# A table of expert gates built two tokens at a time instead of four, in a transformer block on one Trainium2 core

## The chip, the core and the metric

The kernel runs on one core of a Trainium2 chip. The core has a matrix engine (PE, with its weight loads shown as PEld), a vector engine (DVE), a scalar engine (ACT), GpSimd (POOL, here used only to issue DMAs) and a sync engine (SP, which issues the weight loads). Every engine works through its own instructions in order; they wait for each other on semaphores. The metric is the device time of one execution in microseconds, as the median of several runs. Before the change it is 2024.65 us (three runs, 2024.57 to 2025.96).

## What is computed

One transformer block for 256 tokens of width 2048, in float32: a modulated norm, a mixer (attention and a gated recurrence), then a feed-forward layer of 16384 experts of which each token uses 8 x 16 = 128. Only the last part matters here:

```python
q = (hf @ wq).reshape(T, PEER_HEADS, 2, PEER_DQ // 2)
s = jnp.einsum('thpd,hpkd->thpk', q, keys)        # two scores of 128 keys for each head
v1, i1 = lax.top_k(s[:, :, 0], 16); v2, i2 = lax.top_k(s[:, :, 1], 16)
vals, pick = lax.top_k(v1[..., :, None] + v2[..., None, :], 16)   # expert = 128 * i1 + i2
g = jax.nn.softmax(vals, axis=-1)
act = gelu(x_c @ down[e_c]) * g_c                 # for the 128 picked experts of a token
out = act @ up[e_c]
```

## The kernel before

The kernel doesn't gather experts. It multiplies all tokens with all 16384 rows of `down` (32 blocks `d` of 512 experts), takes the gelu, multiplies with a dense gate table that is zero where an expert was not picked, and multiplies the result with all of `up` (16 groups `u`). For this each float32 weight is split into a high and a low part in a shorter format: ACT casts `raw` to `wh` (L209), DVE subtracts to get `wl` (L210), and PE multiplies three times (L375 to L377 for `d`, L358 to L360 for `u`). One such split (128 x 1024 values) and the 24 matmuls of 256 columns (`d`), or 12 of 512 (`u`), that use it are called a round here. There are three buffers each for `wh` and `wl`. So the split for round n can only start when PE has finished round n-3, and runs while PE is in round n-2. Rounds 0 to 31 make the queries `wq`, rounds 32 to 191 are the first 20 `d` blocks (eight rounds each), round 192 is the first of `u`.

The gate table `wd` in DRAM is built by `w_build` while PE works on the first 20 `d` blocks. For each token DVE makes two one-hot rows of 128 (`oh`, L1198), one for each half of the expert number; the first is scaled by the high and low part of the gate (`ga`, by ACT in L1228 and by DVE in L1225); PE multiplies the second with them (`w`, L1218), which gives 128 x 256 sums for a token. These are taken out of PSUM by ACT (L1209, high part) and DVE (L1210, adds the low part) into `stg`, of which there is one buffer. Every 32 tokens `stg` is stored to `wd` by a DMA of 2 MB (L1212, issued by POOL). Each step makes four tokens. A token's sums take half a PSUM bank; there are four banks for them (three with the tag `t`, one with the tag `p`), thus for two steps of four tokens.

The order of work is written by generators. After every round `tick` advances them: a job of priority 0 (the gelu of a `d` block, `ev_d`, two steps, once in eight rounds) comes first; the table has priority 3 and gets the rate in the last place of `RATES` for each round, but in the round in which `ev_d` is at the head, two steps are run, and the second of them runs on into the table. A scheduler then sets each engine's order from priorities and its own durations. Before block 19 (round 184) all steps that are left are emitted, the memory of the table's tiles is given back, and the first two blocks of gates are asked for: `act_load` issues `wt` (gates, read from `wd`, L1250) and `xS` (gelu values stored earlier in `xd`, L1247) on POOL; `act` multiplies them on DVE (L1260, four parts of 128 x 256) and splits the product into `ah` (ACT) and `al` (DVE), which the rounds of `u` need. `xT` and `xS` share three buffers, `wt` has two.

Of the kernel before, what the change touches and what calls it, by code (L numbers as in the profile page):

```python
# [8 lines left out]
F32R = mybir.dt.float32r  # L9
# [3 lines left out]
OP = mybir.AluOpType  # L13
AX = mybir.AxisListType

P = 128
D = 2048
S = 256
# [10 lines left out]
NEB = NE // 512  # L29
NUG = NE // 1024  # L30
LAG = 20
RATES = (2, 1.8, 0.7, 0.51)
WK = 0
ADG = 9
RG = 2
# [15 lines left out]
GPLACE = 48  # L51
# [19 lines left out]
def kernel(  # L71
# [24 lines left out]
    V, A, T, G = nc.vector, nc.scalar, nc.tensor, nc.gpsimd  # L96
# [12 lines left out]
    def ps_t(name):  # L109
        return ps[0].tile([P, 512], F32, tag="t", bufs=ps[2], name=name)  # L110
# [20 lines left out]
    iota = con[:, C_IOTA:C_IOTA + P]  # L131
# [21 lines left out]
    for ch in STREAM.replace(" ", ""):  # L153
# [6 lines left out]
        else:  # L160
            src, o = wid[ch].pop(0)
# [184 lines left out]
    def tick(n=1):  # L346
        tk[0] += min(n, RATES[jobs[0][0]]) if jobs and (jobs[0][0] < 3 or wn[0] > WK) else n
        while tk[0] >= 1:
            tk[0] -= 1
            step()  # L350
# [156 lines left out]
    for which, i0, i1 in SEGS:  # L507
# [11 lines left out]
        if not sums[which]:  # L519
            if which == "f":  # L520
                t = [vp.tile([P, 2, NT, 512], F32, tag="av", bufs=ADAB, name=f"part{i}") for i in range(2)]
                sums["f"] = [[t[b // 2][:, b % 2, tb] for tb in range(NT)] for b in range(4)]
            else:
                t = sqp.tile([P, 4, NT, 512], F32, name="sums")
# [534 lines left out]
    for i in range(8):  # L1059
        t = x1T[:, 2 * i:2 * i + 2]  # L1060
# [19 lines left out]
    kq = e4.enter_context(tc.tile_pool(name="kq", bufs=1))  # L1080
    idT = kq.tile([P, S, 2], F32, name="idT")
# [97 lines left out]
        A.copy(idT[:, tbs[tb]].rearrange("p t i -> p i t"), tp[:, 0:2 * P].rearrange("p (i t) -> p i t", i=2))  # L1179
        A.copy(gT[:, tbs[tb]], tp[:, 2 * P:3 * P])  # L1180

    def turn_tile(tag, place, dt, name):

        t = kq.tile([P, 4 * 2 * P + (64 if place else 0)], dt, tag=tag, bufs=3, name=name)
        return t[:, place:place + 4 * 2 * P].rearrange("p (k o i) -> p k o i", k=4, o=2)

    def w_build():

        stg, ohs, gas, wps = {}, {}, {}, {}
        gl = kq.tile([P, S], F32, name="gl")  # L1190
        gh = kq.tile([P, S], F32R, name="gh")
        A.copy(gh, gT)
        V.tensor_tensor(gl, gT, gh.bitcast(F32), OP.subtract)
        for q in range(64 + 4):
            wn[0] = q
            if q < 64:
                oh = turn_tile("oh", 0, F32R, f"oh{q}")
                V.tensor_tensor(oh, iota.unsqueeze(1).unsqueeze(1).to_broadcast([P, 4, 2, P]),  # L1198
                                idT[:, 4 * q:4 * q + 4].unsqueeze(3).to_broadcast([P, 4, 2, P]), OP.is_equal)
                ohs[q] = oh  # L1200
            if 0 <= q - 4:
                p_, tg = q - 4, (q - 4) // 8
                if p_ % 8 == 0:
                    stg[tg] = kq.tile([P, P, 32], F32, tag="stg", bufs=1, name=f"stg{tg}")
                o = (p_ % 8) * 4
                for k, w in enumerate(wps.pop(p_)):
                    w4 = w.rearrange("p (k o i) -> p i o k", k=2, o=2)
                    d = stg[tg][:, :, o + 2 * k:o + 2 * k + 2]
                    A.copy(d, w4[:, :, 0])  # L1209
                    V.tensor_tensor(d, d, w4[:, :, 1], OP.add)  # L1210
                if p_ % 8 == 7:
                    G.dma_start(wd[tg], stg.pop(tg))  # L1212
            if 0 <= q - 3 < 64:
                p_ = q - 3
                oh, ga = ohs.pop(p_), gas.pop(p_)
                wps[p_] = [ps_t(f"w{p_}0"), (ps_p if p_ % 2 else ps_t)(f"w{p_}1")]
                for k in range(4):
                    T.matmul(wps[p_][k // 2][:, k % 2 * S:k % 2 * S + S], oh[:, k, 1], ga[:, k].rearrange("p o i -> p (o i)"),  # L1218
                             start=True, stop=True)
            if 0 <= q - 1 < 64:  # L1220
                p_ = q - 1
                ga = turn_tile("ga", GPLACE, F32R, f"ga{p_}")
                gas[p_] = ga
                hot = ohs[p_][:, :, 0].bitcast(F32)
                V.tensor_tensor(ga[:, :, 1], hot, gl[:, 4 * p_:4 * p_ + 4].unsqueeze(2).to_broadcast([P, 4, P]), OP.mult)  # L1225
                for k in range(4):
                    t = 4 * p_ + k
                    A.activation(ga[:, k, 0], hot[:, k], AF.Copy, scale=gh[:, t:t + 1].bitcast(F32))  # L1228
            yield

# [69 lines left out]
    for s in range(LAG):  # L1300
        if s == 0:
            finish(0)
            add(picks(0), 2)
            add(picks(1), 2)
            add(w_build(), 3)
        if s == LAG - 1:
            while jobs:
                step()
            e4.close()
            upp = ctx.enter_context(tc.tile_pool(name="upp", bufs=1))  # L1310
            acc = upp.tile([P, NT, D], F32, name="acc")
            for eb in range(2):
                act_load(eb, upp)
                add(act(eb, upp))
        add(ev_d(s, turned(f"d{s}", ticks=2)), 0)
# [124 lines left out]
```

## Time and profile before

| what | value |
|---|---|
| median of three runs | 2024.65 us |
| profiled execution, own time | 2027.09 us |
| its span | 2025.3 us |
| PE busy | 1953.6 us (96%) |
| DVE busy | 1529.3 us (76%) |
| ACT busy | 1024.1 us (51%) |
| POOL busy | 67.6 us (3%) |
| granted PE clock, mean | 0.983 |
| the table's products (L1218), first and last start | 664.4 to 1002.5 us |
| first matmul of `u` | 1057.12 us |

A busy PE is not PE at its peak, since matmuls are pipelined and their ends are modelled. So for PE the starts of the matmuls are read beside the busy share. Idle time of an engine that is not the bottleneck costs nothing; a wait counts when PE waits behind it.

### The profile page before, as it was taken

How to read it: one execution, taken by the hardware profiler on the slowest of the kernel's cores; microseconds unless marked ns; L12 is line 12 of the kernel's file. 1: busy time of each engine (PE TensorE's matmuls, PEld its weight loads, DVE VectorE, ACT ScalarE, POOL GpSimd, SP SyncE). 2: the span in 40 equal slices, each digit the busy share in tenths (PEclk: the TensorE clock that was granted, in tenths of full speed). 3: DMA queues.
4: the chain of work that ended last, by engine and by line, in shares of the span. 5: the costliest groups of instructions: out<-in, count | busy, mean ns of one | idle time of the engine just before them, and what ended most of it. 6: DMA issues, size and time to landing. Idle time of an engine off the chain costs nothing.

```text
span 2025.3 us, 30935 instructions
## 1 busy us (share of the span) xinstructions
PE 1953.6 (96%) x12346; PEld 1728.4 (85%) x12346; DVE 1529.3 (76%) x2342; ACT 1024.1 (51%) x1519; POOL 67.6 (3%) x107
## 2 busy tenths in 40 slices
PE   5999898898999999999999999999999999999998
PEld 4777565787999999999998888888899999999997
DVE  7888999887999888788757666666566666665566
ACT  3544676455445767677654444444344444444442
POOL 0000000000000000000011000000000000000000
PEclk7999998898999999999999999999999999999999
DMA  9898778895546676666798776775577777676563
GB/s 374 325 372 330 277 307 315 345 347 219 175 169 208 215 260 234 229 230 232 270 331 300 246 242 229 234 251 201 190 267 253 262 250 253 240 243 212 190 223 131
DMA packets 77600, 515.39 MB, mean 254 GB/s; under 512 B 8720, under 2 KB 9232, under 8 KB 21904
## 3 DMA queue, kind: packets, MB, share of 16 engines
q1 hardware_dynamic: 63792, 450.50, 62.0%
q0 software_dynamic: 13664, 62.92, 9.0%
q8 instruction: 96, 1.57, 0.3%
q14 instruction: 48, 0.39, 0.1%
HBM read 481.93 MB, written 31.46 MB: 253 GB/s over the span
## 4 chain that ended last, share of the span: by engine, by line
PE 75%; DVE 10%; issue 10%; DMA 3%; ACT 2%; POOL 1%; SPq 0%; DVEq 0%; POOLq 0%
PE u L359 11%; PE u L358 11%; PE u L360 11%; PE d L377 8%; PE d L376 8%; PE d L375 8%; DVE av L231 3%; DVE wl L210 3%; PE wq L375 2%; PE wq L376 2%; PE wq L377 2%; PE y L360 1%; PE y L358 1%; PE y L359 1%; DMA wd<-stg 1%
## 5 line engine op out<-in xcount | busy, mean ns | idle before, releaser
L210 DVE TENSOR_TENSOR wl<-raw,wh 128x1024 fp32r<-128x1024 f32 x649 | 789.3, 1220 | 374.7 <-ACT wh L209 372.0
L209 ACT CAST wh<-raw 128x1024 fp32r<-128x1024 f32 x649 | 680.2, 1051 | 768.5 <-PE u L360 364.2
L377 PE MATMUL d<-xH,wl 128*128 128x256 f32 x2048 | 568.4, 278 | 0.8 <-DVE wl L210 0.7
L375 PE MATMUL d<-xH,wh 128*128 128x256 f32 x2048 | 568.4, 278 | 0.0
L376 PE MATMUL d<-xL,wh 128*128 128x256 f32 x2048 | 567.9, 277 | 0.0
L359 PE MATMUL u<-wl,ah 128*128 128x512 f32 x1024 | 398.9, 390 | 1.3 <-DVE wl L210 1.3
L358 PE MATMUL u<-wh,ah 128*128 128x512 f32 x1024 | 398.7, 389 | 0.0
L360 PE MATMUL u<-wh,al 128*128 128x512 f32 x1024 | 398.4, 389 | 0.0
L377 PEld LDWEIGHTS d<-xH,wl 128*128 128x128 f32 x2048 | 385.3, 188 | 1.3 <-DVE wl L210 1.2
L376 PEld LDWEIGHTS d<-xL,wh 128*128 128x128 f32 x2048 | 385.2, 188 | 0.4
L375 PEld LDWEIGHTS d<-xH,wh 128*128 128x128 f32 x2048 | 385.2, 188 | 0.4
L359 PEld LDWEIGHTS u<-wl,ah 128*128 128x128 f32 x1024 | 192.2, 188 | 41.2 <-DVE wl L210 1.7
L360 PEld LDWEIGHTS u<-wh,al 128*128 128x128 f32 x1024 | 192.3, 188 | 40.2
L358 PEld LDWEIGHTS u<-wh,ah 128*128 128x128 f32 x1024 | 192.2, 188 | 39.7
L231 DVE SCALAR_TENSOR_TENSOR av<-av,cb 128x2048 f32<-128x2048 f32 x64 | 145.8, 2283 | 6.0 <-DMA av<-in_ada_w_dram 6.0
L1198 DVE TENSOR_TENSOR oh<-con,idT 128x1024 fp32r<-128x1024 f32 x64 | 78.1, 1221 | 33.4 <-PE w L1218 33.3
L1228 ACT ACTIVATE ga<-oh,gh 128x128 fp32r<-128x128 f32 x256 | 83.0, 394 | 18.1 <-DVE oh L1198 16.3
L375 PE MATMUL wq<-xH,wh 128*128 128x256 f32 x256 | 73.5, 288 | 2.5 <-ACT xH L209 2.5
L376 PE MATMUL wq<-xL,wh 128*128 128x256 f32 x256 | 73.2, 286 | 0.0
L377 PE MATMUL wq<-xH,wl 128*128 128x256 f32 x256 | 73.0, 285 | 0.0
L1284 DVE TENSOR_TENSOR acc<-acc,u 128x512 f32<-128x512 f32 x112 | 71.5, 679 | 0.0
L1210 DVE TENSOR_TENSOR stg<-stg,w 128x256 f32<-128x256 f32 x128 | 48.3, 421 | 10.3 <-ACT stg L1209 10.3
(363 smaller groups left out, 2080.0 us busy)
## 6 DMA issues: line engine op xcount, KB each, us to landing
raw<-in_down_dram SPq DMA_DIRECT2D x128, 1024.0 KB, 5.6
raw<-in_up_dram SPq DMA_DIRECT2D x128, 1024.0 KB, 5.4
av<-in_ada_w_dram SPq DMA_DIRECT2D x64, 1024.0 KB, 7.1
raw<-in_w_a_dram SPq DMA_DIRECT2D x32, 1024.0 KB, 9.0
raw<-in_ada_p_dram SPq DMA_DIRECT2D x16, 1024.0 KB, 7.1
raw<-in_w_out_dram SPq DMA_DIRECT2D x16, 1024.0 KB, 8.1
raw<-in_wq_dram SPq DMA_DIRECT2D x16, 1024.0 KB, 5.2
wd<-stg POOLq DMA_DIRECT2D x8, 2048.0 KB, 8.4
```

What stands on the lines that cost most here:

```text
L209: A.copy(dst_h, src)
L210: V.tensor_tensor(dst_l, src, dst_h.bitcast(F32), OP.subtract)
L231: V.scalar_tensor_tensor(out=t, in0=t, scalar=1.0, in1=cb, op0=OP.mult, op1=OP.mult, accum_out=m)
L358: T.matmul(o, ah, bh, start=first, stop=False)
L359: T.matmul(o, ah, bl, start=False, stop=False)
L360: T.matmul(o, al, bh, start=False, stop=last)
L375: T.matmul(o, wh[:, kk, ws], bH[:, kc], start=f and i % 2 == 0, stop=False)
L376: T.matmul(o, wh[:, kk, ws], bL[:, kc], start=False, stop=False)
L377: T.matmul(o, wl[:, kk, ws], bH[:, kc], start=False, stop=e and i % 2 == 1)
L1198: V.tensor_tensor(oh, iota.unsqueeze(1).unsqueeze(1).to_broadcast([P, 4, 2, P]), idT[:, 4 * q:4 * q + 4].unsqueeze(3).to_broadcast([P, 4, ...
L1228: A.activation(ga[:, k, 0], hot[:, k], AF.Copy, scale=gh[:, t:t + 1].bitcast(F32))
L1284: V.tensor_tensor(a, a, pst[tb], OP.add)
```

## The change

A step of the table now makes two tokens instead of four, in one PSUM bank instead of two. The rate is 1.04 instead of 0.51 steps for each round. `oh` and `ga` have six buffers of half the size instead of three. A product is emitted four steps after its one-hots (it was three), and its sums are taken out two steps after the product (it was one). `stg` still holds 32 tokens, in one buffer.

```diff
@@ -29,7 +29,7 @@
 NEB = NE // 512
 NUG = NE // 1024
 LAG = 20
-RATES = (2, 1.8, 0.7, 0.51)
+RATES = (2, 1.8, 0.7, 1.04)
 WK = 0
 ADG = 9
 RG = 2
@@ -1179,10 +1179,10 @@
         A.copy(idT[:, tbs[tb]].rearrange("p t i -> p i t"), tp[:, 0:2 * P].rearrange("p (i t) -> p i t", i=2))
         A.copy(gT[:, tbs[tb]], tp[:, 2 * P:3 * P])
 
-    def turn_tile(tag, place, dt, name):
-
-        t = kq.tile([P, 4 * 2 * P + (64 if place else 0)], dt, tag=tag, bufs=3, name=name)
-        return t[:, place:place + 4 * 2 * P].rearrange("p (k o i) -> p k o i", k=4, o=2)
+    def turn_tile(tag, place, name):
+
+        t = kq.tile([P, 2 * 2 * P + (64 if place else 0)], F32R, tag=tag, bufs=6, name=name)
+        return t[:, place:place + 2 * 2 * P].rearrange("p (k o i) -> p k o i", k=2, o=2)
 
     def w_build():
 
@@ -1191,40 +1191,40 @@
         gh = kq.tile([P, S], F32R, name="gh")
         A.copy(gh, gT)
         V.tensor_tensor(gl, gT, gh.bitcast(F32), OP.subtract)
-        for q in range(64 + 4):
+        nq = S // 2
+        for q in range(nq + 6):
             wn[0] = q
-            if q < 64:
-                oh = turn_tile("oh", 0, F32R, f"oh{q}")
-                V.tensor_tensor(oh, iota.unsqueeze(1).unsqueeze(1).to_broadcast([P, 4, 2, P]),
-                                idT[:, 4 * q:4 * q + 4].unsqueeze(3).to_broadcast([P, 4, 2, P]), OP.is_equal)
+            if q < nq:
+                oh = turn_tile("oh", 0, f"oh{q}")
+                V.tensor_tensor(oh, iota.unsqueeze(1).unsqueeze(1).to_broadcast([P, 2, 2, P]),
+                                idT[:, 2 * q:2 * q + 2].unsqueeze(3).to_broadcast([P, 2, 2, P]), OP.is_equal)
                 ohs[q] = oh
-            if 0 <= q - 4:
-                p_, tg = q - 4, (q - 4) // 8
-                if p_ % 8 == 0:
+            if 0 <= q - 6:
+                p_, tg = q - 6, (q - 6) // 16
+                if p_ % 16 == 0:
                     stg[tg] = kq.tile([P, P, 32], F32, tag="stg", bufs=1, name=f"stg{tg}")
-                o = (p_ % 8) * 4
-                for k, w in enumerate(wps.pop(p_)):
-                    w4 = w.rearrange("p (k o i) -> p i o k", k=2, o=2)
-                    d = stg[tg][:, :, o + 2 * k:o + 2 * k + 2]
-                    A.copy(d, w4[:, :, 0])
-                    V.tensor_tensor(d, d, w4[:, :, 1], OP.add)
-                if p_ % 8 == 7:
+                o = (p_ % 16) * 2
+                w4 = wps.pop(p_).rearrange("p (k o i) -> p i o k", k=2, o=2)
+                d = stg[tg][:, :, o:o + 2]
+                A.copy(d, w4[:, :, 0])
+                V.tensor_tensor(d, d, w4[:, :, 1], OP.add)
+                if p_ % 16 == 15:
                     G.dma_start(wd[tg], stg.pop(tg))
-            if 0 <= q - 3 < 64:
-                p_ = q - 3
+            if 0 <= q - 4 < nq:
+                p_ = q - 4
                 oh, ga = ohs.pop(p_), gas.pop(p_)
-                wps[p_] = [ps_t(f"w{p_}0"), (ps_p if p_ % 2 else ps_t)(f"w{p_}1")]
-                for k in range(4):
-                    T.matmul(wps[p_][k // 2][:, k % 2 * S:k % 2 * S + S], oh[:, k, 1], ga[:, k].rearrange("p o i -> p (o i)"),
+                wps[p_] = (ps_p if p_ % 4 == 3 else ps_t)(f"w{p_}")
+                for k in range(2):
+                    T.matmul(wps[p_][:, k * S:k * S + S], oh[:, k, 1], ga[:, k].rearrange("p o i -> p (o i)"),
                              start=True, stop=True)
-            if 0 <= q - 1 < 64:
+            if 0 <= q - 1 < nq:
                 p_ = q - 1
-                ga = turn_tile("ga", GPLACE, F32R, f"ga{p_}")
+                ga = turn_tile("ga", GPLACE, f"ga{p_}")
                 gas[p_] = ga
                 hot = ohs[p_][:, :, 0].bitcast(F32)
-                V.tensor_tensor(ga[:, :, 1], hot, gl[:, 4 * p_:4 * p_ + 4].unsqueeze(2).to_broadcast([P, 4, P]), OP.mult)
-                for k in range(4):
-                    t = 4 * p_ + k
+                V.tensor_tensor(ga[:, :, 1], hot, gl[:, 2 * p_:2 * p_ + 2].unsqueeze(2).to_broadcast([P, 2, P]), OP.mult)
+                for k in range(2):
+                    t = 2 * p_ + k
                     A.activation(ga[:, k, 0], hot[:, k], AF.Copy, scale=gh[:, t:t + 1].bitcast(F32))
             yield
```

On DVE, at the place where `stg` is handed over to its DMA and filled anew (here from the fourth to the fifth 32 tokens), before the change. `w310` and `w311` are the two banks of step 31, `w320` and `w321` those of step 32:

```order
L1210 TENSOR_TENSOR stg3_7866<-stg3_7866,w311_8306 128x128x2
L1225 TENSOR_TENSOR ga34_8388<-oh34_8299,gl_6050 128x4x128
L210 TENSOR_TENSOR wl_8370<-raw_8063,wh_8369 128x1024
L1198 TENSOR_TENSOR oh35_8375<-con_66,idT_3798 128x1024
L210 TENSOR_TENSOR wl_8419<-raw_8139,wh_8418 128x1024
L1225 TENSOR_TENSOR ga35_8465<-oh35_8375,gl_6050 128x4x128
L210 TENSOR_TENSOR wl_8447<-raw_8139,wh_8446 128x1024
L1210 TENSOR_TENSOR stg4_8454<-stg4_8454,w320_8382 128x128x2
L1198 TENSOR_TENSOR oh36_8452<-con_66,idT_3798 128x1024
L210 TENSOR_TENSOR wl_8498<-raw_8221,wh_8497 128x1024
L1210 TENSOR_TENSOR stg4_8454<-stg4_8454,w321_8383 128x128x2
```

And now, with `w63` as the last two tokens of the fourth 32 and `w64` as the first two of the fifth:

```order
L1210 TENSOR_TENSOR stg3_8142<-stg3_8142,w63_8678 128x128x2
L1225 TENSOR_TENSOR ga69_8802<-oh69_8754,gl_6050 128x2x128
L1199 TENSOR_TENSOR oh70_8794<-con_66,idT_3798 128x512
L210 TENSOR_TENSOR wl_8749<-raw_8426,wh_8748 128x1024
L1225 TENSOR_TENSOR ga70_8813<-oh70_8794,gl_6050 128x2x128
L1199 TENSOR_TENSOR oh71_8806<-con_66,idT_3798 128x512
L210 TENSOR_TENSOR wl_8791<-raw_8506,wh_8790 128x1024
L1225 TENSOR_TENSOR ga71_8854<-oh71_8806,gl_6050 128x2x128
L1199 TENSOR_TENSOR oh72_8847<-con_66,idT_3798 128x512
L1199 TENSOR_TENSOR oh73_8892<-con_66,idT_3798 128x512
L210 TENSOR_TENSOR wl_8842<-raw_8506,wh_8841 128x1024
L1210 TENSOR_TENSOR stg4_8796<-stg4_8796,w64_8717 128x128x2
```

In both orders three splits stand between the last addition into the old `stg` and the first into the new one. Before, a one-hot and a split stood between the two banks of step 32; now the additions follow each other.

On POOL, at the end of the table, before the change:

```order
L1240 DMA xd_81<-xT16_10421 128x1024
L1212 DMA wd_82<-stg7_10116 128x4096
L1250 DMA wt0_10919<-wd_82 128x8x128
L1250 DMA wt1_10923<-wd_82 128x8x128
L1240 DMA xd_81<-xT17_10700 128x1024
```

And now on POOL:

```order
L1240 DMA xd_81<-xT17_10861 128x1024
L1247 DMA xS0_11173<-xd_81 128x1024
L1247 DMA xS1_11177<-xd_81 128x1024
L1240 DMA xd_81<-xT18_11154 128x1024
L1212 DMA wd_82<-stg7_10700 128x4096
L1250 DMA wt0_11175<-wd_82 128x8x128
L1250 DMA wt1_11179<-wd_82 128x8x128
```

On PE, at the border of blocks 18 and 19:

```order
L377 MATMUL d18_1_10832<-xH_78,wl_11061 128x256
L1218 MATMUL w125_11146<-ga125_11032,oh125_10986 128x256 x2
L1218 MATMUL w126_11151<-ga126_11073,oh126_11025 128x256 x2
L1218 MATMUL w127_11160<-ga127_11110,oh127_11066 128x256 x2
L375 MATMUL d19_0_11181<-xH_78,wh_11101 128x256
```

The three last products of the table now stand between the last matmul of block 18 and the first of block 19, in front of round 184; before, the last one stood in front of round 172. So the last store of the table has moved from between the stores of blocks 16 and 17 to behind that of block 18.

On DVE, at the first multiplication with gates, before the change (`wl_10952` is the split for round 186):

```order
L210 TENSOR_TENSOR wl_10952<-raw_10732,wh_10951 128x1024
L1260 TENSOR_TENSOR xS0_10917<-xS0_10917,wt0_10919 128x256 x4
L210 TENSOR_TENSOR wl_10986<-raw_10732,wh_10985 128x1024
L1260 TENSOR_TENSOR xS1_10921<-xS1_10921,wt1_10923 128x256
L210 TENSOR_TENSOR al0_10956<-xS0_10917,ah0_10955 128x1024
```

And now (`wl_11340` is the split for round 190, `wl_11368` that for round 191, the last of block 19, and `wl_11398` that for the first of `u`):

```order
L210 TENSOR_TENSOR wl_11340<-raw_11064,wh_11339 128x1024
L1260 TENSOR_TENSOR xS0_11173<-xS0_11173,wt0_11175 128x256
L210 TENSOR_TENSOR wl_11368<-raw_11064,wh_11367 128x1024
L1260 TENSOR_TENSOR xS0_11173<-xS0_11173,wt0_11175 128x256 x3
L1260 TENSOR_TENSOR xS1_11177<-xS1_11177,wt1_11179 128x256 x3
L210 TENSOR_TENSOR wl_11398<-raw_11142,wh_11397 128x1024
L210 TENSOR_TENSOR al0_11212<-xS0_11173,ah0_11211 128x1024
L1260 TENSOR_TENSOR xS1_11177<-xS1_11177,wt1_11179 128x256
L210 TENSOR_TENSOR wl_11426<-raw_11142,wh_11425 128x1024
L210 TENSOR_TENSOR al1_11278<-xS1_11177,ah1_11277 128x1024
L210 TENSOR_TENSOR wl_11454<-raw_11243,wh_11453 128x1024
L1260 TENSOR_TENSOR xS2_11435<-xS2_11435,wt2_11437 128x256 x2
```

The first multiplication now stands four rounds later, in front of the last split that block 19 needs, and the split for the fourth round of `u` follows the last row shown.

## Rows read from the trace of the kernel before

**Rows 1.** Busy time in stretches of 10 us, with PE's granted clock.
```profile
core 0: us, PE busy (x) PEld busy (x) DVE busy (x) ACT busy (x) POOL busy (x), PEclk, DMA share, GB/s
...
810.00:820.00 10.00, 10.00 (x87) 10.00 (x86) 7.67 (x11) 6.70 (x14) 0.53 (x1) 1.00 0.56 185
...
1080.00:1090.00 10.00, 8.72 (x39) 6.88 (x38) 7.18 (x11) 3.35 (x4) 0.89 (x1) 1.00 0.65 187
```

**Rows 2.** What PE waited for from 640 to 1010 us: total, times, longest.
```profile
PE w L1218 <- DVE stg L1210: 2.5, 3, 1.4
PE pkT L1177 <- DVE sel L1172: 1.1, 1, 1.1
```

**Rows 3.** PE in order of time: start, us, engine, line, operation.
```profile
760.48 0.81 PE L1218 MATMUL w<-ga,oh 128*128 128x256 f32 x4 [0.61 <-DVE stg L1210]
...
899.77 0.28 PE L376 MATMUL d<-xL,wh 128*128 128x256 f32 x1
...
901.66 0.28 PE L377 MATMUL d<-xH,wl 128*128 128x256 f32 x1
...
936.33 0.81 PE L1218 MATMUL w<-ga,oh 128*128 128x256 f32 x4 [0.47 <-DVE stg L1210]
...
1002.26 0.62 PE L1218 MATMUL w<-ga,oh 128*128 128x256 f32 x4
...
1007.82 0.28 PE L375 MATMUL d<-xH,wh 128*128 128x256 f32 x1
...
1009.63 0.28 PE L376 MATMUL d<-xL,wh 128*128 128x256 f32 x1
...
1057.12 0.40 PE L358 MATMUL u<-wh,ah 128*128 128x512 f32 x1
```

**Rows 4.** Groups on DVE from 700 to 990 us: count, busy, mean ns, idle before.
```profile
L1198 DVE TENSOR_TENSOR oh<-con,idT 128x1024 fp32r<-128x1024 f32 x54 | 66.0, 1222 | 28.2 <-PE w L1218 28.1
L1210 DVE TENSOR_TENSOR stg<-stg,w 128x256 f32<-128x256 f32 x108 | 40.7, 420 | 10.3 <-ACT stg L1209 10.3
L1225 DVE TENSOR_TENSOR ga<-oh,gl 128x512 fp32r<-128x512 f32 x54 | 36.8, 682 | 0.0
```

**Rows 5.** DMA issues on POOL in order of time.
```profile
704.67 0.53 POOL L1212 DMA_DIRECT2D wd<-stg  x1 [7.48 <-DVE stg L1210]
...
919.44 0.53 POOL L1240 DMA_DIRECT2D xd<-xT  x1 [24.59 <-ACT xT L1237]
924.15 0.53 POOL L1212 DMA_DIRECT2D wd<-stg  x1 [4.18 <-DVE stg L1210]
...
1005.62 0.53 POOL L1212 DMA_DIRECT2D wd<-stg  x1 [12.38 <-DVE stg L1210]
1013.80 1.80 POOL L1250 DMA_DIRECT2D wt<-wd  x2 [7.66 <-ACT xT L1237]
```

**Rows 6.** ACT in order of time.
```profile
712.55 0.40 ACT L1209 COPY stg<-w 128x256 f32<-128x256 f32 x1 [1.97 <-DMA wd<-stg]
...
935.34 0.93 ACT L1209 COPY stg<-w 128x256 f32<-128x256 f32 x3 [2.84 <-DMA wd<-stg]
...
1036.40 0.59 ACT L1237 ACTIVATE xT<-d 128x512 f32<-128x512 f32 x1
```

**Rows 7.** DVE in order of time.
```profile
1004.57 0.75 DVE L1210 TENSOR_TENSOR stg<-stg,w 128x256 f32<-128x256 f32 x2
...
1009.33 1.23 DVE L210 TENSOR_TENSOR wl<-raw,wh 128x1024 fp32r<-128x1024 f32 x1 [1.49 <-ACT wh L209]
1012.04 1.23 DVE L210 TENSOR_TENSOR wl<-raw,wh 128x1024 fp32r<-128x1024 f32 x1 [1.50 <-ACT wh L209]
...
1037.67 1.43 DVE L1260 TENSOR_TENSOR xS<-xS,wt 128x256 f32<-128x256 f32 x4
```

**Rows 8.** Landing of the tile `wt` (990 to 1100 us).
```profile
DMA to landing us min/median/max: 4.9/7.6/8.9
```

**Rows 9.** Landing of the tile `xS` (990 to 1100 us).
```profile
DMA to landing us min/median/max: 4.0/7.7/14.7
```

## The prediction, made before the result was known

> **What bounds the kernel now.** I read first the busy time by stretches, then the waits of PE in the part where the table is built, then the order of time on PE, POOL, ACT and DVE. From 650 to 1055 us PE is the bound: it is busy without a gap in nearly every stretch of 10 us, at a granted clock of 1.00 [rows 1]. For the table it waits 2.5 us in three places, each time for DVE's L1210 [rows 2], which has not yet emptied a PSUM bank because `stg` is still being stored. DVE idles 28.1 us in front of `oh`, waiting for products [rows 4]; nothing of that reaches PE, so the deeper line of one-hots is worth nothing by itself.
>
> PE has two paces in the `d` blocks. From 899.77 to 901.66 us, 16 starts apart, a matmul takes 118.1 ns; from 1007.82 to 1009.63, also 16 apart, 113.1 ns [rows 3], with the same clock. The slow pace began with the wait at 760.48 and ended with the one at 936.33 [rows 3]: 176 us at a loss of 4.2%, or 7.5 us. A wait of PE can thus change the pace in either direction, and I find nothing in the rows that says in which.
>
> A round at the quick pace is 2.71 us (1012.04 - 1009.33, [rows 7]; 24 x 113.1 ns gives the same). `u` starts at 1057.12 [rows 3]; eight rounds earlier, at 1035.4, block 19 began. I count from there as t = 0.
>
> **The rate.** Doubling the rate doesn't keep the speed. In eight rounds the old rate gives 7 x 0.51 = 3.57 steps, and the round with `ev_d` one more: 4.57 steps of four tokens, 18.3 tokens. Now it is 7 x 1.04 + 1 = 8.28 steps of two: 16.6 tokens. The extra step is worth half. The orders say the same: the products stretched from round 62 to 172, and now from 63 to 184, where the rest of the steps is flushed. So the table is complete 12 rounds later, 33 us, and the lead that it had over `u` is what pays.
>
> **First gates, the main term.** In front of t = 0 PE now does six products (0.7 us). ACT takes out the last two banks behind the gelu of block 18, whose second half starts at t + 1.0 (1036.40, [rows 6]) and lasts 0.6; three copies follow, and DVE's last addition ends near t + 3.1. POOL issues the store of `stg` at t + 3.4. Its landing: 7.9 us (704.67 to 712.55), 8.2 (1005.62 to 1013.80, where the first load of gates starts at once) and 11.2 (924.15 to 935.34) [rows 5, 6]. The long one had a store of `xT` 4.7 us ahead of it (919.44); now one stands directly ahead, so I take 11.2. The load of `wt` lands 4.9 to 8.9 us after its issue, 7.6 in the middle [rows 8]. So the gates are there at T = 3.4 + 11.2 + 7.6 = 22.2 (ends 16.2 and 23.5).
>
> Behind this wait DVE has the split for round 191, the last of block 19. PE needs it at 0.7 + 7 x 2.71 + 0.2 = 19.9; it comes at T + 0.35 + 1.2 (a part of the multiplication and a split, 1.43/4 and 1.23 in [rows 7]). Then follow six more parts, a split and the `al` of the first block: T + 6.2. Without a wait PE would ask for that `al` at 0.7 + 8 x 2.71 + 0.5 = 22.9. It gets it at 28.4: 5.5 us lost, between 0 (T at 16.2) and 6.8 (T at 23.5). Before, the first multiplication stood at 1037.67 [rows 7], 19 us ahead of `u`.
>
> **Second gates.** The load of `xS` for block 2 needs the buffer that `al` frees, and stands on POOL behind a load of `wt` that waits for the end of the second multiplication: issue at T + 7.5, landing 4.0 to 14.7 us later, 7.7 in the middle [rows 9]: T + 15.2. DVE has the split for the fourth round of `u` behind two parts of that product: T + 17.1. PE, having started late, asks for it at T + 14.5. That is 2.6 us more (0 to 9.6; I take the middle landing). Later loads of the same kind are late as before: PE already loses 1.3 us at 1080 to 1090 [rows 1], and I leave that as it is.
>
> **Hand-over of `stg`.** From the start of a step's product to the store is 3.4 us before (1002.26, additions from 1004.57, store 1005.62, [rows 3, 5, 7]); one bank less to take out makes it 3.0. Landing 7.9 to 11.2, middle of these ends 9.5; copy, addition and product another 1.0 (935.34 to 936.33, [rows 3, 6]). So the first product that needs a freed bank can go 13.5 us after the last of the old 32 tokens (11.9 to 15.2). In the new order five of the seven hand-overs leave five rounds for it, two leave four (from the product `w63` in front of round 124 to `w68` in front of 128, and from 155 to 159). Five rounds and five products of 0.23 us are 14.7 us: no wait, 0.5 at the worst; four are 12.0: a wait of 1.5 (0 to 3.2). In all 2 x 1.5 + 0.7 = 3.7 us in place of 2.5: +1.2. The old order lost some of its 2.5 because a one-hot and a split stood between the two banks of one step; that goes, and is in this sum.
>
> **What else changes.** The first one-hots are half as long and only one split, not two, stands ahead of the sum for which PE waits 1.1 us in front of L1177 [rows 2]: -1.1. DVE has twice as many one-hots and `ga` products. 1222 ns for 1024 values and 682 for 512 [rows 4] leave some 142 ns that don't shrink with the size; 64 more of each cost DVE 18 us. They are spread over 121 rounds instead of 110, so that DVE's load for a round stays: before 0.58 steps x (1.22 + 0.68 + 2 x 0.42), now 1.06 x (0.68 + 0.42 + 0.42), both 1.6 us, and 1.2 for the split, in 2.95 us of PE. DVE idle of 28 us [rows 4] covers what is left. ACT copies and scales exactly the same pieces. If DVE's cover were gone, splits would come late and PE would lose up to these 18 us; I take 0. The products in smaller groups cost PE nothing: four in a row start on the same beat as the `d` matmuls around them. The pace of PE: its waits are dealt anew. All quick would give back 7.5; slow wherever it was quick from 706 to 760 and 936 to 1057 would cost 175 x 4.4% = 7.7. I take 0, the middle.
>
> The sum is 5.5 + 2.6 + 1.2 - 1.1 + 0 = +8.2 us. The profiled execution took 2027.09, 2.4 above the median of 2024.65; by the median the forecast is 2033 us.
>
> **Rivals.** (1) The lead is still enough: the store lands in 7.9 and the gates in 5.4 or less, T is at most 16.7, and T + 6.2 is in time. Then +1.2 - 1.1 is left: 2025, no change. For it: the last store, at 1005.62, landed in 8.2. Against it: no store next to another transfer of POOL was quick.
>
> (2) Faster: with short pieces the bank is free before PE asks, the waits at `stg` vanish, and PE keeps the quick pace that it has before 760 us. That gives -2.5 - 1.1 - 7.5, and with a tail of 5: -6, or 2019. It decides if all hand-overs land within 10 us. For it: the additions no longer have a split between them. Against it: two hand-overs leave a round less. The Trainium skill (Perfetto Trace Analysis, "Optimizing Scalar/DVE Operations") has this rule: where ACT and DVE are not full but cause gaps on another engine, cutting instructions up can let work finish sooner. By that rule the gaps of 2.5 us would go; the trace agrees with its condition (DVE and ACT below full), but shows that what ends the gap is a DMA, not a long instruction.
>
> (3) Much slower: the first wait sets the slow pace for good (+7.7), both four-round hand-overs wait 3.2 (+3.9 after the 2.5 of before), the gates land at T = 23.5 and `xS` in 10: 6.8 + 5 - 1.1 more. Together +22: 2047.
>
> **How the numbers follow.** The forecast has 0.60 (its own range 2026 to 2041), no change by a lead that is enough 0.18, faster 0.12, much slower 0.10. What a measurement of this kernel can tell from no change is about 0.2%, 4 us. Faster by more: 0.13, from (2) and a little of (1). Within: 0.19, most of (1) and the low end of the forecast. Slower: 0.68. The range that leaves out 2 in 10 goes from 2020, which takes in most of (2), to 2043.
>
> **What would show it.** Right: the table's last product starts beside the first matmul of block 19; POOL's last store of `stg` follows directly behind the store of block 18's gelu; DVE waits for `wt` in front of its first multiplication for several us, and PE waits for L210 in the last round of block 19 or the first of `u`; two waits of PE for L1210 near the fourth and sixth hand-over. Wrong: PE runs from `d` into `u` without a gap; or PE's starts are 113 ns apart throughout and the time falls; or DVE is full and PE waits for splits in the midst of the table.

## The result, and the profile after

The changed kernel takes 2040.78 us (median of four runs, 2037.51 to 2043.82); on the same chip the kernel before takes 2025.31 (four runs, 2024.57 to 2026.15). The ratio is 1.0072, with a 95% interval of 1.0054 to 1.0090: slower by 15.5 us, where +8.2 was forecast. The profiled execution took 2043.82 us (span 2042.1, mean granted clock 0.98). Its 16.8 us over the span of before fall into three parts:

| part of the span | before | after | difference |
|---|---|---|---|
| up to the first `d` matmul | 574.68 | 572.32 | -2.4 |
| from there to the first `u` matmul | 482.44 | 492.32 | +9.9 |
| from the first `u` matmul to the end | 968.2 | 977.5 | +9.3 |

The change touches nothing in the first part. The second holds the table, the third starts with the first gates. What PE waited for in each, from 640 to 1010 us and from 1010 to 1140 (total, times, longest; [rows 2] answers to the first):

```profile
PE w L1218 <- DVE stg L1210: 8.1, 4, 3.5
...
PE u L359 <- DVE wl L210: 6.4, 2, 5.4
PE d L377 <- DVE wl L210: 1.6, 1, 1.6
PE u L360 <- DVE al L210: 0.6, 1, 0.6
```

The hand-overs of `stg` now cost 8.1 us instead of 2.5, and the wait for `pkT` (1.1) is gone. What the waits leave behind is seen in stretches of 10 us (columns as in [rows 1]; the granted clock is the third number from the end):

```profile
720.00:730.00 10.00, 7.84 (x55) 7.68 (x54) 8.03 (x15) 7.11 (x16) 0.00 (x0) 0.83 0.51 193
...
960.00:970.00 10.00, 6.51 (x34) 6.33 (x33) 4.27 (x10) 3.79 (x9) 0.00 (x0) 0.66 0.52 196
...
1070.00:1080.00 10.00, 4.58 (x21) 3.50 (x19) 2.35 (x5) 1.52 (x2) 0.35 (x1) 0.94 0.78 280
1080.00:1090.00 10.00, 10.00 (x33) 7.98 (x34) 9.16 (x15) 5.04 (x5) 3.40 (x5) 0.72 0.88 290
```

Before, the clock in such stretches was 1.00 [rows 1]. PE in order of time at the longest hand-over and behind it:

```profile
960.01 0.28 PE L377 MATMUL d<-xH,wl 128*128 128x256 f32 x1
963.78 0.77 PE L1218 MATMUL w<-ga,oh 128*128 128x256 f32 x2 [3.49 <-DVE stg L1210]
964.35 0.41 PE L375 MATMUL d<-xH,wh 128*128 128x256 f32 x1
964.56 0.41 PE L376 MATMUL d<-xL,wh 128*128 128x256 f32 x1
...
969.25 0.41 PE L377 MATMUL d<-xH,wl 128*128 128x256 f32 x1
...
969.74 0.28 PE L375 MATMUL d<-xH,wh 128*128 128x256 f32 x1
969.85 0.28 PE L376 MATMUL d<-xL,wh 128*128 128x256 f32 x1
```

After 3.49 us without work the matmuls start 213 ns apart (964.35, 964.56), from 969.74 on 113 again: 24 matmuls at the lower level, 1.2 GHz, each about 100 ns late, 2.4 us in all. Behind the wait of 2.15 us at 722.54 another 17 matmuls, from 723.82 to 727.2, run like this: 1.7 us. Behind the waits of 1.43 and 1.00 us (773.02, 913.88) the clock stays at 1.00. The Trainium skill (TensorE: Matmul & The Clock Gate, "What's actually happening") says that the clock has just these two levels and falls when PE idles. The trace agrees on the levels (213 and 113 ns); idling of 1.43 and 1.00 us did not bring the clock down.

The store in front of that wait, on POOL, ACT and DVE:

```profile
950.72 0.53 POOL L1212 DMA_DIRECT2D wd<-stg  x1 [9.76 <-DVE stg L1210]
```
```profile
962.81 1.22 ACT L1209 COPY stg<-w 128x256 f32<-128x256 f32 x4 [3.88 <-DMA wd<-stg]
```
```profile
963.21 1.42 DVE L1210 TENSOR_TENSOR stg<-stg,w 128x256 f32<-128x256 f32 x4 [3.71 <-ACT stg L1209]
```

The landing took 12.1 us (950.72 to 962.81); before, the three stores of [rows 5] took 7.9, 11.2 and 7.5. (The prediction reads 8.2 for the third, up to the issue of the load of gates at 1013.80; but that row names ACT, not the store, as what ended POOL's wait.) Now the end of the table, first POOL, then DVE, then PE:

```profile
1042.15 0.54 POOL L1240 DMA_DIRECT2D xd<-xT  x1 [17.10 <-ACT stg L1209]
1043.92 0.54 POOL L1212 DMA_DIRECT2D wd<-stg  x1 [1.23 <-DVE stg L1210]
1054.18 1.80 POOL L1250 DMA_DIRECT2D wt<-wd  x2 [9.73 <-DMA wd<-stg]
...
1067.68 0.56 POOL L1247 DMA_DIRECT2D xS<-xd  x1
```
```profile
1060.33 0.43 DVE L1260 TENSOR_TENSOR xS<-xS,wt 128x256 f32<-128x256 f32 x1 [6.14 <-DMA wt<-wd]
1060.67 1.22 DVE L210 TENSOR_TENSOR wl<-raw,wh 128x1024 fp32r<-128x1024 f32 x1
...
1077.93 0.76 DVE L1260 TENSOR_TENSOR xS<-xS,wt 128x256 f32<-128x256 f32 x2 [7.65 <-DMA xS<-xd]
1078.61 1.22 DVE L210 TENSOR_TENSOR wl<-raw,wh 128x1024 fp32r<-128x1024 f32 x1
```
```profile
1040.23 0.84 PE L1218 MATMUL w<-ga,oh 128*128 128x256 f32 x6
...
1061.94 0.38 PE L377 MATMUL d<-xH,wl 128*128 128x256 f32 x1 [1.60 <-DVE wl L210]
...
1064.64 0.40 PE L358 MATMUL u<-wh,ah 128*128 128x512 f32 x1
...
1066.23 0.50 PE L360 MATMUL u<-wh,al 128*128 128x512 f32 x1 [0.63 <-DVE al L210]
...
1079.88 0.80 PE L359 MATMUL u<-wl,ah 128*128 128x512 f32 x1 [5.42 <-DVE wl L210]
1080.47 0.63 PE L360 MATMUL u<-wh,al 128*128 128x512 f32 x1
```

The chain is read from DVE: its first multiplication stands idle for 6.14 us until `wt` lands, and the splits behind it (L210 at 1060.67 and 1078.61) are ready, but queued: ACT's casts for them had ended at 1055.7 and 1070.5. PE waits for the first of them in block 19's last round and for the second in the fourth round of `u`. Behind that 5.42 us, too, the clock is down (0.72 in the stretch from 1080): starts 0.43 us apart until 1085.2 where 0.23 is usual, 2.7 us.

The one-hots that were cut in half did not free DVE of its waiting. The groups on DVE from 700 to 990 us ([rows 4] answers):

```profile
L1199 DVE TENSOR_TENSOR oh<-con,idT 128x512 fp32r<-128x512 f32 x95 | 65.4, 691 | 26.9 <-PE w L1218 26.8
L1225 DVE TENSOR_TENSOR ga<-oh,gl 128x256 fp32r<-128x256 f32 x95 | 39.5, 419 | 0.1
L1210 DVE TENSOR_TENSOR stg<-stg,w 128x256 f32<-128x256 f32 x95 | 38.5, 418 | 18.7 <-ACT stg L1209 18.7
```

In front of `oh` DVE still idles 26.8 us for products of PE, as it did before (28.1), now before shorter pieces.

### The profile page after: what moved, and what is told of

Same layout as the page of the kernel before. It is cut to its first block, busy times and chain, and to the rows that moved or that the text cites. A ratio compares the mean times of both kernels' runs of the same rounds, so it can differ in the third digit from the quotient of the medians.

```text
span 2042.1 us, 31031 instructions
## 1 busy us (share of the span) xinstructions
PE 1955.3 (96%) x12346; PEld 1728.3 (85%) x12346; DVE 1547.2 (76%) x2470; ACT 1022.8 (50%) x1519; POOL 67.6 (3%) x107
## 4 chain that ended last, share of the span: by engine, by line
PE 78%; DVE 10%; issue 6%; DMA 4%; ACT 2%; POOL 0%; SPq 0%; DVEq 0%; POOLq 0%; ACTq 0%
PE u L359 11%; PE u L358 11%; PE u L360 11%; PE d L377 9%; PE d L375 9%; PE d L376 9%; DVE av L231 3%; DVE wl L210 2%; DMA wd<-stg 2%; PE wq L375 1%; PE wq L376 1%; PE wq L377 1%; PE y L360 1%; PE y L358 1%; PE y L359 1%
## 5 line engine op out<-in xcount | busy, mean ns | idle before, releaser
L210 DVE TENSOR_TENSOR wl<-raw,wh 128x1024 fp32r<-128x1024 f32 x649 | 790.2, 1222 | 353.5 <-ACT wh L209 344.6
L1199 DVE TENSOR_TENSOR oh<-con,idT 128x512 fp32r<-128x512 f32 x128 | 87.9, 690 | 34.0 <-PE w L1218 33.7
L1228 ACT ACTIVATE ga<-oh,gh 128x128 fp32r<-128x128 f32 x256 | 88.3, 396 | 4.8 <-DVE oh L1199 4.6
## 6 DMA issues: line engine op xcount, KB each, us to landing
wd<-stg POOLq DMA_DIRECT2D x8, 2048.0 KB, 10.8
```

Of the source, the lines that this page charges most:

```text
L210: V.tensor_tensor(dst_l, src, dst_h.bitcast(F32), OP.subtract)
```

## The experiments

Two theories stood against each other. Lateness: the new rate completes the table twelve rounds later, and this makes the time, through the gates and through where the hand-overs fall; the size of a step matters little. Step size: twice as many instructions and shorter hand-overs make it. The runs cross the size (four or two tokens), the lead (last product in front of round 172 to 174, "early", or of 184, "late") and the number of `stg` buffers. Each was timed beside the kernel before, whose medians were 2027.33 us on one chip and 2027.13 on another. The kernel before spreads there from 2019 to 2035 us, so a single time means little; the intervals are what to read.

**Four tokens, but late.** The kernel before with a lower rate, last product in front of round 184.

```diff
-RATES = (2, 1.8, 0.7, 0.51)
+RATES = (2, 1.8, 0.7, 0.449)
```

> The kernel before with steps of four tokens, and only the rate set from 0.51 to 0.449, so that the table's last product stands in front of round 184, as in the changed kernel. Theory (the lead over the first gates is lost, 2.9 us, then the second load of gelu values, 5.6, then 2.6 of a lower clock): 1 to 2 us of wait in the last round of block 19, a long wait in the fourth round of u, together about 11 us behind 1035 us. Hand-overs of stg leave six or seven rounds here, so they should not wait (-2.5) and the pace may stay quick (-7): total between +2 and +11 against the kernel before. Rival (the doubling of the number of small instructions costs the time): no more than +-3, since the pieces are as large as before.

Measured: 2037.12 us, ratio 1.0048 (1.0031 to 1.0066). PE's waits from 640 to 1140 us:

```profile
PE u L359 <- DVE wl L210: 6.2, 3, 5.0
PE w L1218 <- DVE stg L1210: 2.5, 2, 1.7
PE pkT L1177 <- DVE sel L1172: 1.1, 1, 1.1
PE d L377 <- DVE wl L210: 0.9, 2, 0.6
PE u L360 <- DVE al L210: 0.6, 1, 0.6
```

The gates' waits are those of the changed kernel, with steps of four tokens and the hand-overs at 2.5 us as before. So 9.8 us of the 15.5 come without any change of the step. I had expected no wait at the hand-overs; six of the seven stores landed late (11.1 to 12.5 us, in the table below), and two of them held PE up.

**Two tokens, but early.** The changed kernel with a higher rate, last product in front of round 174. All seven hand-overs then leave four rounds.

```diff
-RATES = (2, 1.8, 0.7, 1.04)
+RATES = (2, 1.8, 0.7, 1.163)
```

> The changed kernel with the rate 1.163 instead of 1.04, so that eight rounds build as many tokens as before the change; the last product stands in front of round 174. Theory: no wait between d and u, so the 11 us of the table's end are back; but all seven hand-overs now leave four rounds instead of five, each waits 2 to 4 us and some are followed by 2.7 us of a low clock: 15 to 35 us there instead of 11. Total about +8 to +30 against the kernel before. Rival (small instructions): about as slow as the changed kernel, with waits for splits in the midst of the table and not at the hand-overs.

Measured: 2028.40 us, ratio 1.0009 (0.9993 to 1.0025): no change. For the time lateness was right. Not for the waits: I expected four-round hand-overs to cost 15 to 35 us, and they cost 4.2, with some 1.5 of lower clock behind the longest (granted clock 0.83 from 970 to 980 us):

```profile
PE w L1218 <- DVE stg L1210: 4.2, 3, 2.5
PE u L359 <- DVE wl L210: 1.5, 2, 1.1
```

The stores had landed in 7.5 to 10.7 us, not in 12. A landing goes with the round in front of which the last product of the store stands, even or odd. A 1 MB load of weights serves two rounds. Seven stores each, round number and landing in us:

| kernel | even rounds | odd rounds |
|---|---|---|
| before | 74: 7.9, 102: 7.9, 116: 9.8, 130: 8.9, 158: 7.9 | 89: 10.7, 145: 11.2 |
| after | 108: 9.3, 124: 7.5, 170: 7.5 | 77: 12.7, 93: 12.3, 139: 11.8, 155: 12.1 |
| four, late | 106: 7.8 | 75: 11.4, 91: 11.2, 121: 12.5, 137: 11.8, 153: 11.1, 169: 11.6 |
| two, early | 76: 7.5, 90: 7.5, 104: 8.7, 118: 7.6, 132: 9.1, 146: 9.2, 160: 10.7 | none |

**The changed kernel, one round later.** If the round's parity sets the landing, shifting all steps by one round must move the waits to the other hand-overs: from the first, second, fifth and sixth to the third, fourth and seventh.

```diff
         nq = S // 2
+        yield
         for q in range(nq + 6):
```

> The changed kernel with one empty step in front of the table, so that every hand-over comes one round later (last products 78, 94, 109, 125, 140, 156, 171 in place of 77, 93, 108, 124, 139, 155, 170). Theory: the store of stg is slow (11 to 13 us) when its last product stands in front of an odd round and quick (7.5 to 9.5) in front of an even one, since a weight load of 1 MB serves two rounds; so hand-overs 1, 2, 5 and 6 become quick and don't wait, 3, 4 and 7 slow: 4, with four rounds, waits 3 to 4 us, 3 and 7 wait 1 to 2. Rival (a store is slow because of the store of gelu values next to it, or by chance): landings don't follow the round.

Measured: 2044.43 us, ratio 1.0089 (1.0066 to 1.0111). Landings: rounds 78, 94, 140, 156 in 8.4, 7.6, 7.5, 9.9 us, rounds 109, 125, 171 in 11.7, 12.0, 11.2. PE's hand-over waits from 640 to 1140 us, and ACT's copies at which three stores land (lines one higher here):

```profile
PE w L1219 <- DVE stg L1211: 6.0, 3, 3.4
```
```profile
815.66 0.92 ACT L1210 COPY stg<-w 128x256 f32<-128x256 f32 x3 [3.99 <-DMA wd<-stg]
865.47 1.22 ACT L1210 COPY stg<-w 128x256 f32<-128x256 f32 x4 [3.98 <-DMA wd<-stg]
...
1011.95 0.96 ACT L1210 COPY stg<-w 128x256 f32<-128x256 f32 x3 [3.56 <-DMA wd<-stg]
```

The first two waits went, the third and fourth hand-over wait now (0.87 us at 816.63, 3.41 at 866.45). The sixth, on an even round, still waits 1.74: it landed in 9.9 us, but leaves only four rounds. The seventh landed in 11.2 and held up ACT (3.56), but not PE. So the landing follows the parity, and landing and rounds together make the wait. A store of gelu values close by doesn't decide: in the changed kernel the stores at 708.85 and 759.77 had one 7.5 and 7.7 us behind them and landed late; here those at 712.36 and 759.51 had one 4.8 us behind and were quick. Why an odd round is longer (the store would run against another part of a weight load) is argued, not shown.

This run also shows that the length of a wait alone does not tell what the clock does. Behind 3.41 us it stayed at 1.00; behind 1.87 us, in `u`, it fell (PE's starts, then the stretches of 10 us):

```profile
866.45 0.47 PE L1219 MATMUL w<-ga,oh 128*128 128x256 f32 x2 [3.41 <-DVE stg L1211]
...
1098.88 0.50 PE L359 MATMUL u<-wl,ah 128*128 128x512 f32 x1 [1.87 <-DVE wl L210]
```
```profile
860.00:870.00 10.00, 6.59 (x56) 6.42 (x56) 6.09 (x12) 5.67 (x14) 0.53 (x1) 1.00 0.68 282
1095.00:1105.00 10.00, 8.13 (x29) 6.19 (x28) 7.18 (x10) 2.09 (x2) 0.89 (x1) 0.83 0.60 181
```

**Two buffers of `stg`, changed kernel.** The hand-over's wait is taken away, the lead stays late. To make room, scratch tiles of an earlier stage are put into the same slots; they are done before the table starts.

```diff
-    kt = kq.tile([P, 16, P], F32, tag="stg", bufs=1, name="kt")
+    kt = kq.tile([P, 16, P], F32, tag="stg", bufs=2, name="kt")
-                    stg[tg] = kq.tile([P, P, 32], F32, tag="stg", bufs=1, name=f"stg{tg}")
+                    stg[tg] = kq.tile([P, P, 32], F32, tag="stg", bufs=2, name=f"stg{tg}")
+        eqs = kq.tile([P, 3, hp, TOPK, TOPK], F32, tag="stg", bufs=2, name=f"eqs{tb}")
-                eq = kq.tile(shape, F32, tag="eq", bufs=3, name=f"eq{tb}{o}{hh}")
+                eq = eqs[:, (2 * o + hh) % 3]
-        gl = kq.tile([P, S], F32, name="gl")
+        gl = kq.tile([P, S], F32, tag="hf", bufs=1, name="gl")
```

> The changed kernel with two buffers for stg instead of one (room is made by putting three scratch tiles of the search into the same slots). Theory: the copy into stg never waits for the store, so the 8.1 us of waits at the hand-overs and about 5 us of low clock behind them go; the end of the table is as late as before and still costs about 11: +3 to +8 against the kernel before, 8 to 12 less than the changed kernel. Rival (small instructions): within 3 us of the changed kernel.

Measured: 2026.72 us, ratio 1.0003 (0.9983 to 1.0024). I had expected it to stay some us slower than before: the hand-overs with all that hangs on them were worth 17 us by the medians (16 by the ratios), not 13. PE's waits from 640 to 1140 us, and stretches of the table (compare the counts of matmuls):

```profile
PE u L359 <- DVE wl L210: 6.0, 2, 4.5
PE d L377 <- DVE wl L210: 2.3, 1, 2.3
```
```profile
860.00:910.00 50.00, 50.00 (x444) 50.00 (x443) 44.10 (x69) 35.78 (x76) 2.13 (x4) 1.00 0.72 254
...
1040.00:1090.00 50.00, 41.70 (x193) 34.49 (x192) 32.88 (x51) 19.38 (x20) 9.51 (x13) 0.93 0.85 287
```

No hand-over waits, and PE keeps the quick pace all through the table, 444 matmuls in 50 us. The kernel before has 427 in the same stretch, at the slow pace:

```profile
860.00:910.00 50.00, 50.00 (x427) 50.00 (x426) 41.41 (x54) 35.44 (x76) 1.60 (x3) 1.00 0.66 233
```

The waits for the gates are still there (8.3 us, and the clock at 0.93 behind them).

**Two buffers of `stg`, kernel before.** The same edit, without the line of `gl`, on steps of four tokens, early.

> The kernel before with two buffers for stg. Theory: its 2.5 us of waits go, and with them the changes of pace that such a wait can bring: PE may keep 113 ns from 625 us to the end of the d blocks, which gives another 7: -2 to -10 against the kernel before. Rival (stg is not what the waits come from): no change.

Measured: 2016.50 us, ratio 0.9966 (0.9940 to 0.9992). The profile has one wait of 1.2 us for L210 and one of 1.2 for `pkT`, and the quick pace throughout. Of its twelve runs nine lie from 2012.88 to 2021.05 us, three from 2032.25 to 2034.17; the profile is of one of the nine, and no trace shows what the three did. So the gain is 10.8 us by the medians, 6.9 by the ratio, which counts all twelve, with an interval of 1.6 to 12: by the middle of either more than the 2.5 us of hand-over waits, though the interval's low end is below them.

**Two tokens, early, two buffers of `stg`.** Both edits on the changed kernel.

> Steps of two tokens at the rate 1.163 (the table as early as before the change) and two buffers for stg. Theory: neither the end of the table nor the hand-overs cost anything, and the size of a step itself is worth nothing: within 3 us of the kernel with four tokens and two buffers, that is 8 to 13 below the kernel before. Rival (small instructions cost PE time): more than 4 us slower than that kernel.

Measured: 2014.42 us, ratio 0.9935 (0.9915 to 0.9955), the lowest median; its interval overlaps that of the kernel with four tokens and two buffers. Of PE's waits from 640 to 1140 us one line is left:

```profile
PE u L359 <- DVE wl L210: 1.8, 1, 1.8
```

**Four tokens, late, two buffers of `stg`.** The rate of 0.449 and the second buffer on the kernel before.

> Steps of four tokens at the rate 0.449 (last product in front of round 184) and two buffers for stg. Theory: only the late end of the table is left; PE waits 1 to 3 us at the end of block 19 and 4 to 6 in the fourth round of u, with a low clock behind it: 8 to 12 above the kernel with the rate 0.51 and two buffers, so between -4 and +2 against the kernel before, as the two-token kernel with two buffers. Rival (it is the two-token order that makes the end dear): within 3 us of the kernel with the rate 0.51 and two buffers.

Measured: 2023.59 us, ratio 0.9984 (0.9971 to 0.9997). The gates' waits are back (4.6 and 0.6 us, the clock at 0.93 from 1040 to 1090), the pace is quick.

**The changed kernel again**, unchanged, as the eighth corner on the same chip.

> The changed kernel itself, on the chip of the other runs. Both theories: +10 to +17 against the kernel before; the waits at hand-overs 1, 2, 5 and 6 are there again (landings near 12), and those in the last round of block 19 and the fourth round of u, if they are fixed by the order and not by chance.

Measured: 2043.80 us, ratio 1.0081 (1.0058 to 1.0104). Its hand-overs wait 2.10, 1.99, 0.61 and 4.22 us at the same four places. The clock falls only behind the last, so a wait of about 2 us does not always bring it down (behind 2.15 at the first hand-over it had fallen).

The eight corners, medians in us:

| | one `stg` | two `stg` |
|---|---|---|
| four tokens, early | 2027.1 to 2027.3 (before) | 2016.5 |
| two tokens, early | 2028.4 | 2014.4 |
| four tokens, late | 2037.1 | 2023.6 |
| two tokens, late | 2043.8 (after) | 2026.7 |

The intervals of the ratios are 3 to 5 us to either side, so differences of 3 us are not told from zero. Read down: with an early end, the step's size changes +1.3 and -2.1 us, not told from zero. Being late costs 9.8 (four tokens) and 15.4 (two) with one buffer, 7.1 and 12.3 with two. Read across: the second buffer gives 11 to 17 us in every row. By the ratios, the 2016.5 of the first row, with its three long runs, counts as 2020.4: then the second buffer gives 7 us there, and a late end 4 us to four tokens with two buffers. With one buffer a late end also moves the hand-overs to other rounds, so the column with two prices the late gates best. With one buffer a late two-token kernel loses 6.7 us more than a late four-token one: its hand-overs wait 8.1 instead of 2.5 us. With two buffers, where they don't wait, 3.1 are left.

## Why the prediction was too low

- **The rate** was right: the last product stands at 1040.23, in front of round 184, and the four-token kernel slowed to the same round loses 9.8 us without any other edit.
- **First gates** were right in mechanism, too large in size. Predicted T = 22.2, measured 20.1 (first multiplication at 1060.33, the products in front of block 19 from 1040.23); the store took 9.7 us in place of 11.2, and the gates were there 6.2 us after their load's issue in place of 7.6. The prediction's own formula gives 3.4 us of loss for T = 20.1. The loss by PE's starts is 2.9 us (1.77 before 1061.94, 1.13 up to 1066.23) instead of 5.5.
- **Second gates** were too small: `xS` issued at 1067.68 was there at 1077.93, 10.2 us in place of the middle 7.7. PE lost 5.6 us at 1079.88, and 2.7 more to the lower clock. Both gates together: 11.2 instead of 8.1.
- **Hand-over of `stg`** is the term that failed: "Landing 7.9 to 11.2, middle of these ends 9.5", with two waits of 1.5, +1.2 in all (a further 0.7 stands in that sum without a source). Measured are +5.6 of waits and 4.1 of lower clock behind two of them (1.7 and 2.4). The formula itself holds: with the landings that were measured (12.7, 12.3, 11.8, 12.1) start plus 3.0, landing and 1.0, against 14.7 for five rounds, or 12.5 for the four of the sixth at the slow pace that PE had there (the prediction's 12.0 is at the quick one), gives waits of 2.0, 1.6, 1.1 and 3.6; the trace has 2.15, 1.43, 1.00 and 3.49. So the error is the landing. Its rows showed two classes, and I took their middle for all; the new order moved four of seven hand-overs into the long class, where before it was two. The waits came at the first, second, fifth and sixth, not at the fourth and sixth as forecast; the fourth leaves four rounds, but its store landed in 7.5. And that a wait is followed by a lower clock had no term: no row of before showed one of that length.
- **The wait for `pkT`** went, -1.1, as predicted. **The pace** was put at 0: slow for 140 us instead of 176, -1.6. **The smaller instructions** cost DVE 17.9 us (busy 1547.2 in place of 1529.3; 18 was predicted) and PE nothing that can be told from zero, as predicted (two tokens, early: ratio 1.0009, 0.9993 to 1.0025).
- The sum for the `d` blocks is 5.6 + 4.1 - 1.1 - 1.6 + 1.8 (the wait in the last round) = 8.8 of 9.9 measured; for `u` 1.1 + 5.6 + 2.7 + 0.9 (a wait at 1097.38) - 1.3 (the wait of before that is gone) = 9.0 of 9.3. The first part's -2.4 is not explained; 1.1 and 0.3 stay open.
- That the time still fell into the range is partly luck. The hand-overs came out 8.5 us above their term and the second gates 5.7, together 14.2; the first gates (2.6 less), the pace (1.6 less) and the 2.4 of the first part made up for some of it.
- Of the rivals, "a lead that is enough" is refuted by DVE's wait for `wt`; the sentence against it, that no store next to another transfer of POOL was quick, is wrong: before the change the stores at 789.62 and 964.54, each with a store of `xT` 4 us behind it, landed in 7.9. Of "much slower", the `xS` landing of 10 (10.2) and one long four-round wait (3.49) came, the slow pace for good did not. "Faster" failed by its own condition (landings within 10 us), but its price was near: without the hand-over waits, by a second buffer, the kernel before gains 10.8 us by the medians and 6.9 by the ratio, where -2.5 - 7.5 = -10 was argued. The rule of the Trainium skill that stood beside it (Perfetto Trace Analysis, "Optimizing Scalar/DVE Operations": cutting instructions up may let work finish sooner) brought nothing here: cut in half at the same lead, the time stays (ratio 1.0009, 0.9993 to 1.0025). What PE's gaps at `stg` hung on was a DMA.

## What to carry to other kernels

If a background job is emitted at a rate per round, changing the size of its step changes when it ends: compute the last round first, and look at what reads its result. A single buffer that is stored by a DMA is worth its landing's spread: read the landings one by one, against the phase of what else loads, rather than their middle. Count a wait of the busiest engine with what follows it, here a lower clock or a slower pace; a second buffer took away 2.5 us of waits and gained 7 by the ratio and 11 by the medians, with an interval of 1.6 to 12.

## What the runs showed that I had not expected

- The same 2 MB store lands in 7.5 to 10.7 us if its last product stands in front of an even round (23 stores of the six executions with one buffer), and in 10.7 to 13.4 if in front of an odd one (19 stores). In the four with two buffers it is 7.5 to 11.0 (16 even) and 10.9 to 14.5 (12 odd): there the two classes touch, so parity is not all of it.
- Behind a wait of PE the granted clock was sometimes lower: 1.7 us lost behind 2.15, 2.4 behind 3.49, 2.7 behind 5.42; none behind 2.10 and 1.99 in another execution, none behind 3.41 and some behind 1.87 in the shifted kernel. What decides it stays open.
- PE's matmuls of 256 columns start 113 or 118 ns apart at a granted clock of 1.00. In all four kernels with two buffers of `stg`, without a hand-over wait, the table ran at 113 throughout. In the kernel shifted by one round the quick pace (443 matmuls from 720 to 770 us) gave way after the wait at 816.63 (342 in 40 us from 820 to 860). What in a wait switches it stays open.
